# A hybrid decoder layer: operand sums of a branch stored by its attention blocks, and half of a projection's tiles computed as pairs

## The chip, the cores and the metric

The kernel runs on one core of a Trainium2 chip. A core has TensorE (PE, matrix products into the eight banks of PSUM), VectorE (DVE), ScalarE (ACT), GpSimd (POOL) and SyncE (SP), which issues most of the DMA transfers. Each engine executes its own list of instructions in order; semaphores order them among each other. The metric is the device time of one execution in microseconds (us). The time before is 2460.73 us, the median of three runs (2457.89 to 2463.26).

## The reference, cut to what matters

One inference step of a layer on 512 prompt tokens and 8 x 4 sample tokens, 544 columns in all, with a model width of 2048:

```
u = einsum('btd,dc->btc', x, w_in)                       # one wide input projection, cut into parts
q_m, k_m, v_m, o_m, z_m, q_a, k_a, v_a, z_a, g_m, g_a, i_pre, f_pre = parts(u)
h_m = mlstm(q_m, k_m, v_m, i_pre, f_pre)                 # 4 heads of 512, matrix memory; also C, n, m
h_a = sliding_window_attention(q_a, k_a, v_a, sinks)     # 32 heads of 64, window 128
br_m = norm(h_m) * gate(o_m, z_m)                        # branch m
br_a = h_a * silu(z_a)                                   # branch a
y = sig(g_m) * (br_m @ w_proj_m) + sig(g_a) * (br_a @ w_proj_a)
out = layernorm(alpha * x + y @ w_out)
```

The outputs are those of prompt and samples, the new mLSTM state and the last keys and values. The change concerns `br_a @ w_proj_a`, how its operand comes about, and mLSTM, which runs beside it.

## The kernel before

Activations stand transposed: a tile holds 128 model rows on the partitions and T = 544 token columns, 16 such tiles for the width. A product in fp32 precision is made of three matmuls with operands split into a high part (fp32r) and the rest: wh x xh, wh x xl, wl x xh. `split` makes wh on ScalarE (L200) and wl on VectorE (L201) of a loaded weight tile of 128 x 1024; `hilo` does the same with an operand (L245, L246).

There are two ways to compute 256 output rows. Plain (`gemm`, `products`): each tile of 128 output rows takes 16 blocks of the width, three products, two halves of 272 columns, 96 matmuls at L210 into two banks. Paired (`paired`, `half_product`): two tiles together by Strassen's scheme (Winograd's form) over halves of the width, of the columns and of the outputs, seven half products of 16 matmuls at L685 and 8 at L687 instead of eight; it needs four sums of the operand's quarters (s1, n2, n3, s4, made by `operand_sums`) and four of the weights' (`prepare`, L665), and its banks are gathered into the outputs (`gather`, L695 to L714).

The program's stages in order of time: x is loaded and transposed; the input projection runs in pairs up to 1754 us, and beside it, as generators that `tick()` advances by a step after each half product, attention (16 blocks k, each one 128 rows of branch a, written to the DRAM tensor d_bra) and the samples' mLSTM. Then `branch(d_bra, ...)` loads the 16 rows of branch a and splits them into the tiles bh and bl, and a loop over ct = 0 to 15 computes the 16 tiles of w_proj_a, all plain; each is multiplied by the gate's tile (L1560) and stored to d_t. Beside it `mlstm` runs on the prompt's four heads, a generator that is advanced after every second block of a plain tile. Behind mLSTM (from 2010 us) the operand of branch m is loaded and split. From 2122 us w_proj_m is computed with merging, two tiles plain and the rest in pairs, and last w_out.

Of one head of mLSTM these lines matter. `values` (L1417) transposes v and splits it into vh, vl. `decays` (L1449) spreads the decay row over the partitions and makes the exponentials dm on ScalarE (L1458), for which an activation table is loaded. `keys` (L1425) transposes k, VectorE weights it (f, L1427), `hilo` splits it to kwh and kwl, and 24 matmuls at L1438 sum one of four parts of the new state C. `cells` makes the scores (L1470), multiplies them by dm into ph and pl, sums the numerators (L1483) of four row blocks, each into a pair of banks, and `layernorm_rows` normalizes them (its last step reads the banks on ScalarE, L1076); transposes (L1493) and a multiplication by the gate end in d_brm.

What sets the order: the program's text is traced by a scheduler that places instructions on each engine's list by priority (`tc.high_priority`) and by explicit successions (`tc.issue_after`); generators interleave by the number of their yields. The pools set what may overlap: psB (tag sm) and psA (tag bank) have four PSUM banks each.

Of the kernel before, what the change touches and what calls it, by code (L numbers as in the profile page):

```python
# [74 lines left out]
def _build(tc, nc, i, o, es):  # L75
# [3 lines left out]
    def pool(stack, name, bufs, space=None, side=None):  # L79
        kw = {"space": space} if space is not None else {}  # L80
        if space is None:
            kw["side"] = side or "right"
            kw["reuse_waits"] = "tile"
        return stack.enter_context(tc.tile_pool(name=name, bufs=bufs, **kw))
# [9 lines left out]
    psB = pool(es, "psB", 4, PSUM)  # L94
    psA = pool(es, "psA", 4, PSUM)

    dr = pool(es, "dr", 1, bass.MemoryType.DRAM)
# [3 lines left out]
    def nm(s):  # L101
        count[0] += 1
        return f"{s}_{count[0]}"

# [71 lines left out]
    d_y = dr.tile([16, 128, T], F32, name="d_y")  # L176
    d_o = dr.tile([12, 128, T], F32, name="d_o")
# [46 lines left out]
    def gemm(wv, c0, xh, xl, cols=EVEN, raws=(None, None), every=8, prio=0, before=None, parts=(1, 1),  # L224
             ps=None, behind=None):
        ps = ps or mm()
        for half in range(2):
# [9 lines left out]
            products(ps, half, wh, wl, xh, xl, cols, every)  # L237
# [480 lines left out]
    def paired(work, plain=None):  # L718
# [6 lines left out]
        for at, (w, n) in enumerate(steps):  # L725
# [11 lines left out]
            if n == 2 and "early" in w:  # L737
                w["early"]()
            half_product(w, n)
# [22 lines left out]
    def kv_head(kvh):  # L762

# [6 lines left out]
        nc.sync.dma_start(vraw, d_vr[0:SEQ, kvh * 64:kvh * 64 + 64].rearrange("(b p) c -> p b c", p=128))  # L770
        k1, k2 = btile("b1", [128, SEQ], "k1", F32R), btile("b1", [128, SEQ], "k2", F32R)
# [5 lines left out]
    def attention(k, qs, sz, kv):  # L777
# [39 lines left out]
        for a in range(2):  # L817
# [16 lines left out]
            yield  # L834
        for a in range(2):
# [13 lines left out]
        nc.sync.dma_start(d_bra[k][:, 0:SEQ], hT[:])  # L849

# [38 lines left out]
    def attentions():  # L889
# [15 lines left out]
        for k in range(16):  # L905
            if k % 4 == 0:
                kv = kv_head(k // 4)
# [16 lines left out]
    def sample_attention():  # L924
# [118 lines left out]

        PTs = weightsT(0)
# [11 lines left out]
        nc.sync.dma_start(d_bra[:, :, SEQ:T].rearrange("k p t -> p k t"), gas[:])  # L1056

    def layernorm_rows(n, den, em, parts, hn, w):
# [11 lines left out]
        G.tensor_tensor(out=s[:, 5:6], in0=s[:, 4:5], in1=mh[:n, 0:1], op=ALU.pow)  # L1070
# [43 lines left out]
    def sample_prep(h, r):  # L1114
# [72 lines left out]
        A.copy(num, pN[:NS, :])  # L1187
        r.update(kv=load_kv(h, 0), den=den, num=num, qs=qs)
# [23 lines left out]
    def sample_head(h):  # L1212
# [12 lines left out]
        for b in range(NB):  # L1225
# [10 lines left out]
            for j in range(7 if h + b == 0 else 4 + b % 2):  # L1236
# [130 lines left out]
    def branch(src, p, tmp, ahead=()):  # L1367

        hs, los = act_tiles(p, "bh"), act_tiles(p, "bl")

        def steps():
            for k in range(KT):
# [5 lines left out]
                hilo(st[:], hs[k // 4][:, k % 4], los[k // 4][:, k % 4])  # L1378
# [3 lines left out]
    _, bah, bal, g_ = branch(d_bra, act, lambda k: ev(), ahead)  # L1382
# [18 lines left out]
    def f5(dt=F32):  # L1401
        return wA2.tile([128, 512], dt, tag="f5", name=nm("f"))

# [18 lines left out]
    def keys(h, c, kt):  # L1422
# [12 lines left out]
        for b in range(4):  # L1435
            for n, (a, b_) in enumerate(((kwh, vh), (kwh, vl), (kwl, vh))):
                for f, pp in enumerate((p0, p1)):
                    PE.matmul(pp[:, 0:258], a[:, b * 128:b * 128 + 128], b_[:, b, f],  # L1438
# [3 lines left out]
        V.tensor_copy(co[:, 256:512], p1[:, 0:256])  # L1442
# [19 lines left out]
    def cells(h, kh, kl, qh, ql):  # L1462
        hns = []
        for bs_ in ((0,), (1,), (2, 3)):
            for b in bs_:
                n = SEQ - b * 128
                pp = sm()
                for c in range(4):
                    for m, (x_, y_) in enumerate(((kh, qh), (kh, ql), (kl, qh))):
                        PE.matmul(pp[:, 0:n], x_[c][:, b * 128:b * 128 + 128], y_[c][:, b * 128:SEQ],  # L1470
# [4 lines left out]
            yield  # L1475
        for js in ((0, 1), (2,), (3,)):
            for j in js:
                p0, p1 = sm(), sm()
                for b in range(j + 1):
                    off = POFF[b] + (j - b) * 128  # L1480
                    for n, (x_, y_) in enumerate(((ph, vh), (ph, vl), (pl, vh))):
                        for f, pp in enumerate((p0, p1)):
                            PE.matmul(pp[:, 0:258], x_[:, off:off + 128], y_[:, b, f],  # L1483
# [3 lines left out]
                hns.append(hn)  # L1487
            yield
        gt = load4(d_g, h)
# [16 lines left out]
    def mlstm():  # L1506
        for h in range(MH):
            vts = load4(d_v, h)
            spawn(decays(h))
            yield  # L1510
            kts = load4(d_k, h)
# [3 lines left out]
            kh, kl, qh, ql = [], [], [], []  # L1515
            g_ = None
            for c in range(4):
                a, b_ = t5(F32R), t5(F32R)
                V.tensor_copy(a[:], kts[c][:])
                V.tensor_tensor(out=b_[:], in0=kts[c][:], in1=r32(a[:]), op=ALU.subtract)  # L1520
                kh.append(a)
                kl.append(b_)
                n_ = keys(h, c, kts[c])
                next(n_)
                if g_ is not None:
# [4 lines left out]
            for c in range(4):  # L1530
# [449 lines left out]
```

## Time and profile before

| | |
|---|---|
| median of three runs | 2460.73 us (2457.89 to 2463.26) |
| the profiled execution | 2460.73 us, span 2459.0 us |
| mean granted TensorE clock | 0.999 |
| TensorE busy | 2444.3 us (99%), 19466 instructions |
| VectorE busy | 1875.3 us (76%) |
| ScalarE busy | 1217.2 us (50%) |
| GpSimd busy | 510.8 us (21%) |
| bytes moved by DMA | 464.72 MB, 169 GB/s of HBM traffic over the span |

A row of the profile's timeline begins with its start and length in us, then come engine, line, operation, the tiles written and read, their shapes and the count of like instructions; brackets show how long the engine had been idle and what released it. Matmuls are pipelined, and a single one is shown with some 0.28 us; the rate is taken from the starts of a run of them. "L685" is the line of the kernel before; the lines of the changed kernel differ, since text is added ahead of them (L210 becomes L218, L245 L253, L1425 L1472, L1438 L1485, L1483 L1533).

### The profile page before, as it was taken

To read this page: it belongs to the slowest core of one execution; us is meant where nothing else is said; L and a number is where in the kernel's file an instruction comes from. 1 tells how busy PE (TensorE), PEld (TensorE's weight loads), DVE (VectorE), ACT (ScalarE), POOL (GpSimd) and SP (SyncE) were. 2 spreads that over 40 slices of the span, in tenths; PEclk is the share of its full clock that TensorE was granted. 3 is DMA by queue.
4 is the path that set the end of the run, shared out by engine and by line. 5 is a ranking of instruction groups with operands and counts; after the bars stand their busy time and mean duration, and the time that the engine had idled before them with its cause. 6 is when DMAs were issued, how large, how long until landed. Compare 5 with 4: busy or idle time off the path is not lost.

```text
span 2459.0 us, 48851 instructions
## 1 busy us (share of the span) xinstructions
PE 2444.3 (99%) x19466; PEld 2382.7 (97%) x19466; DVE 1875.3 (76%) x2810; ACT 1217.2 (50%) x1999; POOL 510.8 (21%) x479
## 2 busy tenths in 40 slices
PE   8999999999999999999999999999999999999999
PEld 8999999999999999999999999999999999999997
DVE  7778888888888887887877888777865654777656
ACT  6456676676676565443433434434633333344431
POOL 4114334334333330211111221211000000110111
PEclk9999999999999999999999999999999999999999
DMA  6876666666666654577677586676755546888876
GB/s 177 205 173 157 161 162 147 161 163 148 160 156 160 155 153 110 153 226 242 182 252 240 162 246 211 192 228 217 248 175 171 185 155 204 226 222 247 220 221 188
DMA packets 555804, 464.72 MB, mean 189 GB/s; under 512 B 43704, under 2 KB 452584, under 8 KB 555320
## 3 DMA queue, kind: packets, MB, share of 16 engines
q1 hardware_dynamic: 538968, 402.88, 55.5%
q0 software_dynamic: 15696, 57.15, 12.1%
q8 instruction: 153, 2.51, 0.4%
q10 hardware_dynamic: 912, 1.57, 0.2%
q14 instruction: 75, 0.61, 0.1%
HBM read 319.06 MB, written 96.31 MB: 169 GB/s over the span
## 4 chain that ended last, share of the span: by engine, by line
PE 98%; DMA 1%; SPq 1%; DVE 0%; ACT 0%; issue 0%; DVEq 0%; ACTq 0%
PE bank L685 47%; PE bank L687 23%; PE bank L210 13%; PE sm L1438 2%; PE sm L210 1%; PE bank L1250 1%; PE sm L1470 1%; PE sm L795 1%; PE sm L1483 1%; PE sm L841 1%; PE sm L1801 1%; PE sm L821 1%; PE sm L1255 1%; PE bank L409 0%; PE bank L1923 0%; DMA raw<-in_w_in 0%
## 5 line engine op out<-in xcount | busy, mean ns | idle before, releaser
L200 ACT CAST wh<-raw 128x1024 fp32r<-128x1024 f32 x632 | 662.6, 1048 | 843.3 <-PE bank L685 695.7
L201 DVE TENSOR_TENSOR wl<-raw,wh 128x1024 fp32r<-128x1024 f32 x632 | 791.7, 1253 | 201.4 <-ACT wh L200 184.1
L685 PE MATMUL bank<-xk,wh 128*128 128x272 f32 x2336 | 322.0, 289 | 0.0
L665 DVE TENSOR_TENSOR raw<-raw,raw 128x1024 f32<-128x1024 f32 x238 | 301.2, 1267 | 6.6 <-DMA raw<-in_w_in 2.6
L685 PEld LDWEIGHTS bank<-xk,wh 128*128 128x128 f32 x2336 | 302.8, 188 | 2.0 <-issue 1.5
L704 POOL TENSOR_TENSOR ev<-p,ev 128x272 f32<-128x272 f32 x82 | 118.3, 1442 | 437.7 <-ACT ev L703 404.7
L687 PE MATMUL bank<-xk,wl 128*128 128x272 f32 x1168 | 170.1, 288 | 0.0
L685 PE MATMUL bank<-s1h,wh 128*128 128x272 f32 x656 | 169.6, 291 | 0.0
L685 PE MATMUL bank<-n2h,wh 128*128 128x272 f32 x656 | 169.6, 291 | 0.0
L685 PE MATMUL bank<-n3h,wh 128*128 128x272 f32 x656 | 169.3, 290 | 0.2 <-ACT wh L200 0.2
L685 PE MATMUL bank<-n2l,wh 128*128 128x272 f32 x656 | 167.7, 287 | 0.0
L685 PE MATMUL bank<-n3l,wh 128*128 128x272 f32 x656 | 167.6, 288 | 0.0
L685 PE MATMUL bank<-s4h,wh 128*128 128x272 f32 x656 | 167.6, 289 | 0.0
L685 PE MATMUL bank<-s1l,wh 128*128 128x272 f32 x656 | 167.3, 287 | 0.0
L685 PE MATMUL bank<-s4l,wh 128*128 128x272 f32 x656 | 167.0, 287 | 0.0
L687 PEld LDWEIGHTS bank<-xk,wl 128*128 128x128 f32 x1168 | 155.7, 188 | 0.1
L685 PE MATMUL bank<-a11h,wh 128*128 128x272 f32 x584 | 150.3, 289 | 0.0
L685 PE MATMUL bank<-a11l,wh 128*128 128x272 f32 x584 | 149.5, 288 | 0.0
L210 PE MATMUL bank<-bl,wh 128*128 128x272 f32 x704 | 147.6, 288 | 0.0
L210 PE MATMUL bank<-bh,wl 128*128 128x272 f32 x704 | 147.5, 290 | 0.0
L210 PE MATMUL bank<-bh,wh 128*128 128x272 f32 x704 | 147.2, 288 | 0.0
L663 POOL DMA_DIRECT2D raw<-raw x90 | 78.3, 871 | 292.5 <-DVE ev L712 211.6
(506 smaller groups left out, 5679.2 us busy)
## 6 DMA issues: line engine op xcount, KB each, us to landing
raw<-in_w_in SPq DMA_DIRECT2D x296, 512.0 KB
raw<-raw POOLq DMA_DIRECT2D x90, 512.0 KB, 4.9
C<-in_state_mlstm_C SPq DMA_DIRECT2D x32, 1024.0 KB
out<-C SPq DMA_DIRECT2D x64, 512.0 KB
raw<-in_w_proj_a SPq DMA_DIRECT2D x32, 512.0 KB
raw<-in_w_proj_m SPq DMA_DIRECT2D x32, 512.0 KB
raw<-in_w_out SPq DMA_DIRECT2D x32, 512.0 KB
d_v<-ev SPq DMA_DIRECT2D x16, 272.0 KB
```

Of the source, the lines that this page charges most:

```text
L200: state["cast"] = A.copy(wh[:, k:k + n], raw[:, k:k + n])
L201: state["split"] = V.tensor_tensor(out=wl[:, k:k + n], in0=raw[:, k:k + n], in1=r32(wh[:, k:k + n]), op=ALU.subtract)
L210: PE.matmul(ps[f][:, :w], a[:, kk], b(k, c, w), start=(k == 0 and n == 0), stop=(k == 15 and n == 2))
L663: G.dma_start(out=w[out][:], in_=w[b][:], accum_op=ALU.add)
L665: V.tensor_tensor(out=w[out][:], in0=w[a][:], in1=w[b][:], op=ALU.add)
L685: PE.matmul(ps, wh[:, k], x(p, k), start=(first and k == 0 and p == 0), stop=False, skip_group_check=True)
L687: state["end"] = PE.matmul(ps, wl[:, k], x(0, k), start=False, stop=(k == 7), skip_group_check=True)
L704: G.tensor_tensor(out=c22, in0=p1, in1=c11, op=ALU.subtract)
L795: PE.matmul(pp[:, c0 + w0:c0 + 256], qs[a][:, j * 128:j * 128 + 128], kx[:, k0:k0 + 256 - w0], start=(n == 0), stop=(n == 1))
L821: PE.transpose(pt[:, b * 128:b * 128 + 128], s_[:, b, 128:256], ident)
L841: PE.matmul(po[:, b * 128:b * 128 + n], VA[:, b], p_[:, 2 * b:2 * b + n // 128], start=(b == 0 and m == 0), stop=(b == 3 and m == 1), skip ...
L1438: PE.matmul(pp[:, 0:258], a[:, b * 128:b * 128 + 128], b_[:, b, f], start=(b == 0 and n == 0), stop=(b == 3 and n == 2))
```

## The change

1. Attention blocks 8 to 15 load the stored row k - 8 (`sc`), form the four operand sums of the prompt's first and last 240 columns of each half (`branch_sums`: four operations of 128 x 240 on VectorE) and store them to d_sa; the remaining columns, those of the samples and 32 beside, are summed once in the samples' chain and stored to d_ss. The keys and values of the next attention head are loaded one block earlier (`kv_load`).
2. Of w_proj_a the tiles 0 to 5 run plain beside mLSTM, 6 and 7 plain behind it, 8 to 13 as three pairs, 14 and 15 plain. `stored_sums` loads the sums by GpSimd's queue, seven ahead, and splits them (sumh, suml) while 6 and 7 run. The plain tiles beside mLSTM have one pair of banks (psA 2, psB 6); before the pairs the pools return to 4 and 4. Branch m's operand is loaded and split behind the pairs.
3. In mLSTM the next head's v and k are loaded while a head's cells run, the high parts of k are cast on ScalarE instead of VectorE, q is split beside the keys, both read-outs of C run on ScalarE, and the output rows are a generator of their own (`rows_out`). The splits of branch a all stand behind the weights of the last input pair.
4. y's operand sums have three buffers instead of two, and PSUM pools wait by tile.

```diff
+    def psum_pools(n):
+        return pool(esPS, nm("psB"), n, PSUM), pool(esPS, nm("psA"), 8 - n, PSUM)
...
-    def paired(work, plain=None):
+    def paired(work, plain=None, rest=()):
...
+            if at == 4:
+                for _ in rest:
+                    pass
...
+        if k in (3, 7, 11):
+            bp["kv"] = kv_load(k // 4 + 1)
+        if k > 7:
+            sc = scores_tile()
+            nc.sync.dma_start(sc[:, 0:4:2, 0:PC], d_bra[k - 8].rearrange("p (c x) -> p c x", c=2)[:, :, 0:PC])
...
         nc.sync.dma_start(d_bra[k][:, 0:SEQ], hT[:])
+        if k > 7:
+            spawn(branch_sums(sc[:, :, 0:PC], hT[:, 0:PC], hT[:, HT:SEQ], d_sa[k - 8]))
...
+    def branch_sums(t_, r12, r22, to):
+        r11, s1, r21, s4 = (t_[:, j] for j in range(4))
+        V.tensor_tensor(out=s1, in0=r22, in1=r21, op=ALU.subtract)
+        V.scalar_tensor_tensor(r21, r11, -1.0, r21, op0=ALU.mult, op1=ALU.subtract)
+        V.tensor_tensor(out=r11, in0=r11, in1=s1, op=ALU.subtract)
+        V.tensor_tensor(out=s4, in0=r12, in1=r11, op=ALU.subtract)
+        nc.sync.dma_start(to, t_)
+        yield
...
-                    nc.sync.dma_start(st[:], src[k])
-                hilo(st[:], hs[k // 4][:, k % 4], los[k // 4][:, k % 4])
+                    nc.sync.dma_start(st[:], src[k])
+                with tc.issue_after(state["cast"].ins), tc.issue_after(state["split"].ins):
+                    hilo(st[:], hs[k // 4][:, k % 4], los[k // 4][:, k % 4])
...
+    esPS.close()
+    psB, psA = psum_pools(6)
...
         A.copy(co[:, 0:256], p0[:, 0:256])
-        V.tensor_copy(co[:, 256:512], p1[:, 0:256])
+        A.copy(co[:, 256:512], p1[:, 0:256])
...
-                V.tensor_copy(a[:], kts[c][:])
-                V.tensor_tensor(out=b_[:], in0=kts[c][:], in1=r32(a[:]), op=ALU.subtract)
-                kh.append(a)
-                kl.append(b_)
+                two_parts(kts[c], (kh, kl))
                 n_ = keys(h, c, kts[c])
                 next(n_)
+                if c > 1:
+                    two_parts(qts[c - 2], (qh, ql))
...
-    for ct in range(16):
-        sg = c5t()
-        nc.sync.dma_start(sg[:], d_sga[ct])
-        ps = gemm(wa_, ct * 128, bah, bal, every=2)
...
+    def stored_sums(to, p):
...
+        def load(n):
+            t_ = two((tx.tile([128, T], F32, tag="tx", name=nm("tx")) if n % 7 < 4 else ev())[:])[:, :, 0:PC]
+            j = n // 8 * 2
+            G.dma_start(out=t_, in_=d_sa[n % 8][:, j:j + 2])
+            return t_
+
+        with tc.issue_after(state["head"].ins):
+            ahead = [load(n) for n in range(7)]
...
+        for n in range(16):
+            for _ in range(2 if 8 <= n < 12 else 1):
+                yield
+            k, t_ = n % 8, ahead.pop(0)
+            to_ = e if n < 8 else f
+            behind_weights(t_, *(t[k // 4][:, k % 4, :, 0:PC] for t in to_))
+            if k == 4:
+                columns(to_)
...
+            if n + 7 < 16:
+                ahead.append(load(n + 7))
...
+    LEAD_A, PAIR_A, TAIL_A = 6, 8, 14
+    marks = []
+    for ct in range(LEAD_A):
+        marks.append(state.get("cells"))
+        with tc.issue_after(marks[ct - 1].ins) if ct > 1 and marks[ct - 1] else ExitStack():
+            plain_a(ct, every=(1, 2), prio=0 if ct else AHEAD)
+    drain()
...
+    sums_ = stored_sums(SA, act3)
+    next(sums_)
+    spawn(sums_)
+    for ct in range(LEAD_A, PAIR_A):
+        with tc.issue_after(state["cells"].ins):
+            plain_a(ct, every=2, prio=AHEAD)
+    esPS.close()
+    psB, psA = psum_pools(4)
+    XA = operands((bah_, bal_), SA)
+    paired([pair_a(ct) for ct in range(PAIR_A, TAIL_A, 2)], state["split"], rest=sums_)
...
+    for ct in range(TAIL_A, 16):
+        plain_a(ct, every=2, prio=AHEAD)
...
-    tx = pool(esT, "txd", 2)
+    tx = pool(esT, "txd", 3)
     Y = {}
-    spawn(operand_sums(d_y, Y, act3))
+    spawn(operand_sums(d_y, Y, act3, 3))
```

How it moves instructions is shown at three places. First TensorE at the first key matmuls of head 0, before; L210 are products of w_proj_a (bank 21460 and 21461: its tile 1), L1438 the key matmuls, L1425 the transposes of the next k.

```order
L210 MATMUL bank_21461<-bh_21103,wh_21643 128x272
L210 MATMUL bank_21460<-bl_21107,wh_21643 128x272
L210 MATMUL bank_21461<-bl_21107,wh_21643 128x272
L1438 MATMUL sm_21366<-vh,kwh_21335 128x258
L1438 MATMUL sm_21367<-vh,kwh_21335 128x258
L1438 MATMUL sm_21366<-vl,kwh_21335 128x258
L1425 MATMUL sm_21413<-cc,t_21214 128x128 x4
```

The same place after; bank 21244 and 21245 are tile 0, bank 21538 is tile 1.

```order
L218 MATMUL bank_21244<-bh_21173,wl_21353 128x272
L218 MATMUL bank_21245<-bh_21173,wl_21353 128x272
L1485 MATMUL sm_21440<-vh,kwh_21408 128x258
L1485 MATMUL sm_21441<-vh,kwh_21408 128x258
L1485 MATMUL sm_21440<-vl,kwh_21408 128x258
L1485 MATMUL sm_21441<-vl,kwh_21408 128x258
L1472 MATMUL sm_21487<-cc,t_21294 128x128 x4
L218 MATMUL bank_21538<-bh_21167,wh_21542 128x272
```

The key matmuls moved from the middle of tile 1 to the end of tile 0: 96 product matmuls now stand ahead of them in this stage, 154 before. Second, ScalarE ahead of the first kwh (t: high parts of k and q; vh: of v; dm: the exponentials), before:

```order
L200 CAST wh_21643<-raw_21641 128x1024
L1458 ACTIVATE dm<-f_21228,colT_90 128x128 x6
L245 CAST t_21538<-t_21316 128x512
L245 CAST vh<-sm_21296 128x4x128
L245 CAST t_21542<-t_21318 128x512
L245 CAST kwh_21335<-f_21333 128x512
```

and after:

```order
L253 CAST t_21552<-t_21296 128x512
L253 CAST vh<-sm_21368 128x4x128
L1500 COPY f_21327<-sm_21324 128x384
L1505 ACT_TABLE_LOAD
L1505 ACTIVATE dm<-f_21326,colT_90 128x128 x4
L253 CAST t_21567<-t_21391 128x512
L1505 ACTIVATE dm<-f_21327,colT_90 128x128 x6
L253 CAST t_21608<-t_21393 128x512
L253 CAST kwh_21408<-f_21406 128x512
```

Between the last bh of branch a and the first kwh ScalarE's list now holds seven casts t instead of two. Third, TensorE where a plain tile follows a plain tile with nothing between, before (banks 24320, 24321, then 24467, 24468: two pairs of the four banks):

```order
L210 MATMUL bank_24320<-bh_21104,wl_24384 128x272
L210 MATMUL bank_24321<-bh_21104,wl_24384 128x272
L210 MATMUL bank_24467<-bh_21101,wh_24471 128x272
L210 MATMUL bank_24468<-bh_21101,wh_24471 128x272
L210 MATMUL bank_24467<-bl_21105,wh_24471 128x272
```

and after (tile 6 in banks 23982 and 23983, tile 7 begins in 24134; the pool has two banks):

```order
L218 MATMUL bank_23982<-bh_21173,wl_24057 128x272
L218 MATMUL bank_23983<-bh_21173,wl_24057 128x272
L218 MATMUL bank_24134<-bh_21167,wh_24138 128x272
L218 MATMUL bank_24134<-bl_21168,wh_24138 128x272
L218 MATMUL bank_24134<-bh_21167,wl_24139 128x272
```

Tile 7 begins with one half alone, in one of the two banks that tile 6 has just filled.

163 lines of the change are left out of this document (116 added, 47 removed).

## The prediction

> **What bounds the kernel now.** I read the page first: the span, the engines' busy time, and the chain that ended last by engine and line.
>
> ```profile
> span 2459.0 us, 48851 instructions
> PE 2444.3 (99%) x19466; PEld 2382.7 (97%) x19466; DVE 1875.3 (76%) x2810; ACT 1217.2 (50%) x1999; POOL 510.8 (21%) x479
> PE 98%; DMA 1%; SPq 1%; DVE 0%; ACT 0%; issue 0%; DVEq 0%; ACTq 0%
> PE bank L685 47%; PE bank L687 23%; PE bank L210 13%; PE sm L1438 2%; PE sm L210 1%; PE bank L1250 1%; PE sm L1470 1%; PE sm L795 1%; PE sm L1483 1%; PE sm L841 1%; PE sm L1801 1%; PE sm L821 1%; PE sm L1255 1%; PE bank L409 0%; PE bank L1923 0%; DMA raw<-in_w_in 0%
> ```
>
> TensorE is the path: 98% of the chain, 70% of it pair matmuls (L685, L687) and 13% plain tiles (L210). Two things can therefore move the time: how many matmuls there are, and new waits of TensorE. Next the list of TensorE's waits (in total, times, longest), then the busy time of each engine in four stretches.
>
> ```profile
> PE sm L295 <- DMA cc<-in_consts: 3.4, 1, 3.4
> ...
> PE sm L1255 <- DMA VB<-d_kv: 1.9, 1, 1.9
> PE bank L210 <- DVE wl L201: 1.3, 1, 1.3
> ```
> ```profile
> 400.00:800.00 400.00, 400.00 (x3222) 400.00 (x3221) 333.86 (x497) 267.62 (x507) 147.17 (x113) 1.00 0.66 156
> 1740.00:1770.00 30.00, 30.00 (x242) 29.95 (x242) 25.95 (x39) 20.51 (x34) 1.49 (x3) 1.00 1.00 331
> 1770.00:2010.00 240.00, 240.00 (x1913) 237.98 (x1912) 144.78 (x373) 85.94 (x168) 12.35 (x18) 1.00 0.49 161
> 2010.00:2125.00 115.00, 115.00 (x923) 114.97 (x922) 69.69 (x121) 42.80 (x68) 5.31 (x7) 1.00 0.75 228
> ```
>
> The columns behind the length are PE, PEld, DVE, ACT, POOL, granted clock, DMA share, GB/s. In the stage that the change rewrites (1755 to 2122) TensorE never waits; VectorE works 60% of it and ScalarE 36%. So there is nothing to win there but matmuls, and every new wait is a loss. The chain gives the rate of TensorE in long pieces:
>
> ```profile
> 1756.58 13.71 PE bank L210 x110
> ...
> 1803.50 1.45 PE sm L1483 x12
> ...
> 1820.93 1.09 PE sm L1493 x10
> ...
> 2012.45 109.59 PE bank L210 x878
> ```
>
> A product matmul takes 109.59/878 = 0.1248 us, a numerator matmul 0.121, a transpose 0.109.
>
> **The matmuls removed: -9.0 us.** A plain tile is 16 blocks x 3 products x 2 halves = 96 matmuls. Two of them become a pair of 7 half products of 24, 168 in all, of the same 272 columns. Three pairs save 3 x 24 = 72 matmuls, 72 x 0.1248 = 9.0 us. All else that TensorE does keeps its count. Nothing excludes that these matmuls count in full: the chain is TensorE there.
>
> **h0's first key matmuls: +4.0 us.** Head 0 of mLSTM now runs beside 96 product matmuls before its first key matmul, where it had 154, counted in the order of the instructions (110 of them are the chain's piece at 1756.58).
>
> When TensorE gets there: the last pair's matmuls are over when the first transposes of before start,
>
> ```profile
> 1754.37 0.60 PE L1417 MATMUL sm<-cc,t 128*128 128x128 f32 x4
> ```
>
> then 96 x 0.125 + 24 transposes x 0.109 + the decay row of about 0.3 = 15.0 us: 1769.4. When kwh is ready: ScalarE works in order, and these are its rows of before.
>
> ```profile
> 1750.55 2.29 ACT L245 CAST bh<-pf 128x544 fp32r<-128x544 f32 x4 [1.95 <-PE bank L685]
> 1752.74 1.04 ACT L200 CAST wh<-raw 128x1024 fp32r<-128x1024 f32 x1
> ...
> 1759.57 0.65 ACT L1310 ACTIVATE ev<-ev 128x544 f32<-128x544 f32 x1
> 1761.91 1.05 ACT L200 CAST wh<-raw 128x1024 fp32r<-128x1024 f32 x1 [1.69 <-issue]
> 1762.90 1.57 ACT L245 CAST vh<-sm 128x512 fp32r<-128x512 f32 x3
> 1766.22 0.48 ACT L1453 COPY f<-sm 128x384 f32<-128x384 f32 x1 [1.75 <-DVE f L1451]
> 1766.72 1.28 ACT L1458 ACT_TABLE_LOAD   x1
> 1768.01 1.28 ACT L1458 ACTIVATE dm<-f,colT 128x128 f32<-128x128 f32 x4
> ...
> 1770.14 1.86 ACT L1458 ACTIVATE dm<-f,colT 128x128 f32<-128x128 f32 x6
> 1771.90 0.60 ACT L245 CAST t<-t 128x512 fp32r<-128x512 f32 x1
> ...
> 1773.41 1.14 ACT L245 CAST kwh<-f 128x512 fp32r<-128x512 f32 x2
> ```
>
> By the order after, ahead of kwh stand seven operand casts t (two before) and four more casts of bh, which before ran earlier, between the last pair's products:
>
> ```profile
> 1737.37 1.81 ACT L245 CAST bh<-pf 128x544 fp32r<-128x544 f32 x3
> ```
>
>  The first four bh fit into the 1.95 us idle and the slot at 1750.55, the next wh ends near 1752.4, then: 4 bh, 4 bh, sigmoid, wh, 4 bh, sigmoid (3 x 2.2 + 2 x 0.6 + 1.0 = 8.8, to 1761.2), 4 t, 2 vh, wh, vh, t, vh (5 casts of t at 0.55, 4 of vh at 0.52, 1.0: 5.8, to 1767.0), copy and table load (1.8, to 1768.8), the exponentials with a t between and one behind (1.2 + 1.8 + 1.1, to 1772.9), kwh 0.55: 1773.4. The wait is 1773.4 - 1769.4 = 4.0 us. Bounds: if the first four bh end 0.9 us earlier, at 1750.6, and TensorE comes 0.6 later by small waits of its own, 2.5; if they get no early slot, the list ends at 1774.8 (5.4). I take the sum itself: it leaves ScalarE no idle time, as the rows of before with their two idles of 1.7 us don't. Tile 1 can't fill in: its bank is one of only two in this stage, and VectorE reads it out behind the f that feeds kwh.
>
> One rule speaks against this term. In the rows above the table load occupies 1.28 us and the next exponential starts 1.29 us after its start, so I sum 1.28. The Trainium skill ("ScalarE: Activation LUTs", What ACT_TABLE_LOAD costs) adds a drain of about 1.38 us to every switch; with it the wait would be an estimated 5.4 us and the time 2459.3. The rows show the copy ahead starting 0.50 us before the load, so no such drain; the rows decide.
>
> **Numerators of head 3: +1.0 us.** Heads 0 to 2 have 21 to 27 product matmuls ahead of their last numerator; head 3 has none: 60 matmuls (6, 12, 18 and 24 for the four row blocks) in a row, each block with two of six banks. Block 3 needs block 0's pair back. It starts 36 x 0.121 = 4.4 us after block 0, whose matmuls take 0.7, and whose banks ScalarE reads last:
>
> ```profile
> 1801.71 0.41 PE L1483 MATMUL sm<-vh,pl 128*128 128x258 f32 x2
> ```
> ```profile
> 1805.57 1.02 ACT L1076 ACTIVATE t<-sm,lns 128x256 f32<-128x256 f32 x2 [3.56 <-DVE lns L1072]
> ```
>
> From the last matmul to free banks: 1806.6 - 1802.0 = 4.6. So 0.7 + 4.6 - 4.4 = 0.9, and a semaphore: 1.0 (0 if block 0's chain is quicker without other work; 2 if a wl of 1.2 falls into it).
>
> **Tile to tile on two banks: +1.2 us.** The plain tiles of this stage own one pair of banks, where they had two. After, tile 7 stands right behind tile 6 and wants its first bank, which VectorE must read out first:
>
> ```profile
> 1768.83 0.78 DVE L1560 TENSOR_TENSOR c<-bank,c 128x272 f32<-128x272 f32 x2
> ```
>
> One read is 0.4, with the matmul's drain and semaphores some 0.8 (0.4 to 1.6, if a wl is in the way). At the other joints mLSTM's matmuls stand between; 0.4 for all of them.
>
> **Costed at nothing.** The eight blocks' sums: 32 operations of 240 columns on VectorE, eight loads and eight stores on SyncE's queue.
>
> ```profile
> L342 DVE TENSOR_TENSOR r<-sm,r 128x240 f32<-128x240 f32 x8 | 3.2, 394 | 0.0
> ```
>
> 4 x 0.39 = 1.6 us for a block; VectorE is 84% busy there (333.86 of 400), so it stays under 88% and the weights stay ahead. If that cover is gone, each block costs up to 1.6, 12.6 in all. Waits they add: the first sum waits on VectorE for GpSimd's last product of the block, and weight parts queue behind it. The 20 splits of stored sums (ScalarE 0.55, VectorE 0.62 each) run beside tiles 6 and 7, 24 us of TensorE, with VectorE's own 15 us of weights and reads there. Sixteen key casts and sixteen read-outs go from VectorE to ScalarE, which has 64% free. A third buffer for y's tiles, the sample chain's moved steps (two earlier, two fewer later) and the key loads moved ahead change no order on TensorE.
>
> Sum: -9.0 + 4.0 + 1.0 + 1.2 = -2.8. The profiled execution took 2460.73 us (span 2459.0), which is the median too (2457.89 to 2463.26): 2457.9. About 0.2%, 4.9 us, is what a measurement of this kernel can tell from no change.
>
> **Rivals.**
> *The waits don't come:* kwh early enough and banks free, so all 72 matmuls are won: 2451.7; with half of the waits 2454.8. For it: no wait at all in this stage before. Against: ScalarE's list is in order and longer by nine casts. 0.27.
>
> *The wait halves the clock.* After the first 3.4 us without work TensorE was slow, after 3.0 us later it was not:
>
> ```profile
> 3.44 4.53 PE L295 MATMUL sm<-cc 128*128 128x128 f32 x20 [3.44 <-DMA cc<-in_consts]
> 7.76 2.14 PE L328 MATMUL sm<-cc,xr 128*128 128x128 f32 x16
> 9.74 0.60 PE L331 MATMUL bank<-cc,xs 128*128 128x128 f32 x4
> 13.33 0.63 PE L328 MATMUL sm<-cc,xr 128*128 128x128 f32 x4 [2.99 <-DMA xr<-in_x_prompt]
> 13.71 0.37 PE L210 MATMUL bank<-a11h,wh 128*128 128x272 f32 x1
> ```
> ```profile
> 0.00:10.00 10.00, 6.56 (x39) 1.00 0.85 235
> ```
>
> 20 transposes in 4.32 us (0.216 each), then 16 in 1.98 (0.124); behind the wait of 2.99, 4 in 0.38. The granted clock (1.00 in the second fence, PE alone) doesn't show it; the spacing does. A wait of 4.0 lies beyond both; slow matmuls for 4.3 us would cost 2.2 more: 2460.1. 0.12. The Trainium skill ("TensorE: Matmul & The Clock Gate", Part 1) has the same rule with a window of about 3.4 us; the trace agrees at both rows.
>
> *Stored sums late, slower:* the first pair's second half product needs half of the sums, read back by GpSimd's queue seven ahead. A load like them:
>
> ```profile
> tx<-d_brm POOLq DMA_DIRECT2D x8, 544.0 KB, 7.2
> ...
> tx<-d_y POOLq DMA_DIRECT2D x8, 544.0 KB, 5.3
> ```
>
> Two rounds of loads are 14.4 us of the 24 that tiles 6 and 7 cover. If the loads start 15 us late, 5 us of them and the splits behind (5 us) stand open: 2468. It ends slower from 7.7 us in the open. For it: a buffer frees only when both engines have split it, and VectorE has the pair's weights too. 0.21.
>
> **How the numbers follow.** Forecast 0.40, its own range 2455 to 2461; waits away 0.27; clock 0.12; sums late, or the same in the attention blocks, 0.21. Faster by over 0.2% (under 2455.8): 0.26 from the waits away and 0.08 from the forecast, 0.34. Slower (over 2465.6): 0.19. Between: 0.47. The range reaches to the first rival's end, 2451.5, and into the last, 2466.0.
>
> **What would show it.** In the changed profile: 72 fewer product matmuls; a wait of TensorE at L1485 on kwh of 2.5 to 5.4 us and of no other head; waits of about 1 us at L1533 and L218; TensorE's spacing behind the first wait (0.125 or 0.25); no wait at the first pair's L693 on suml. Wrong would be: waits of TensorE in the attention blocks, at the first pair, or a chain with less than 97% of TensorE.

## The result, and the profile after

The changed kernel takes 2472.87 us (median, 2471.99 to 2474.5) where the kernel before, run beside it, takes 2459.4 (2457.89 to 2463.26): a ratio of 1.0048, with an interval of 1.0036 to 1.006. It is half a per cent slower. The forecast was 2457.9 with a range up to 2466.0, so it was wrong, and on the wrong side. The two profiled executions differ in the same way: spans of 2471.1 and 2459.0 us, 12.1 apart. The page after, its lines on the span, the engines and the chain:

```profile
span 2471.1 us, 48979 instructions
PE 2443.2 (99%) x19394; PEld 2379.0 (96%) x19394; DVE 1903.9 (77%) x2857; ACT 1247.9 (50%) x2069; POOL 523.2 (21%) x504
PE 91%; issue 3%; DMA 3%; DVE 2%; ACT 0%; SPq 0%; POOL 0%; ACTq 0%; DVEq 0%; POOLq 0%
```

The 72 matmuls are gone (19466 before, 19394 now), and yet TensorE's busy time is only 1.1 us shorter, where 72 x 0.1248 is 9.0: the matmuls that are left are in part slower ones. Its share of the chain has fallen from 98% to 91%. The list of TensorE's waits (in all, times, longest) says who took its place:

```profile
PE sm L1297 <- DMA VB<-d_kv: 5.7, 2, 3.3
PE sm L1485 <- issue: 3.5, 1, 3.5
...
PE sm L994 <- DMA kb<-in_state_attn_k: 1.7, 1, 1.7
PE bank L218 <- DVE wl L209: 1.4, 2, 1.2
PE sm L1212 <- DVE nT L1208: 0.9, 1, 0.9
PE sm L1533 <- ACT t L1116: 0.9, 1, 0.9
PE sm L1485 <- ACT kwh L253: 0.7, 2, 0.5
...
PE bank L218 <- DVE c L1694: 0.5, 1, 0.5
```

They fall into two places. L1485 (keys), L1533 (numerators) and L218 belong to w_proj_a with mLSTM beside it, where the forecast looked. L994 (the samples' attention), L1212, a further 0.6 at L1225 and the first of the two waits at L1297 (all the samples' mLSTM) lie between 898 and 1061 us, in the input projection, where it costed everything at nothing.

Aligning the pair matmuls of both traces by their number gives the account: +0.1 us up to 898 us, **+10.0 between 898 and 1061**, +0.9 from there to the last input pair, +0.1 from 1754 to 2100 (9.0 of matmuls gained, 9.1 of waits and slow clock lost), +1.9 for two waits on wl at 2104.8 and 2117.3, -1.5 since the wait on wl that the kernel before has at 2294 is gone, +0.6 behind the last matmuls. The sum is 12.1. Five sixths of the loss thus come from one stretch of 163 us.

This is how TensorE passes the worst place there, the samples' matmuls with VB. Its timeline before (start, length, line, tiles, count):

```profile
1047.16 0.50 PE L1255 MATMUL sm<-VB,Ab 32*128 32x512 f32 x4
1047.59 0.39 PE L685 MATMUL bank<-n3h,wh 128*128 128x272 f32 x1
...
1050.71 0.29 PE L685 MATMUL bank<-s4h,wh 128*128 128x272 f32 x1
```

and after:

```profile
1054.59 0.88 PE L1297 MATMUL sm<-VB,Ab 32*128 32x512 f32 x4 [3.27 <-DMA VB<-d_kv]
1055.40 0.59 PE L693 MATMUL bank<-n3h,wh 128*128 128x272 f32 x1
...
1060.79 0.29 PE L693 MATMUL bank<-s4h,wh 128*128 128x272 f32 x1
```

The load of VB comes 3.27 us late. Behind it the 24 matmuls with n3 take 5.39 us (1055.40 to 1060.79) where they took 3.12 before (1047.59 to 1050.71), and the four with VB 0.81 instead of 0.43: 2.7 us more, for a clock that fell during the wait. Busy time and granted clock in windows of the same trace (length, PE busy, clock, DMA share, GB/s):

```profile
1055.00:1062.00 7.00, 7.00 (x38) 0.61 0.91 273
1785.00:1788.00 3.00, 3.00 (x17) 0.58 0.44 128
```

**Why VB is late.** VB holds what an earlier step of the samples' chain stored, so its load is the last link of a chain of transfers. SyncE's timeline at the start of that chain, before:

```profile
1006.26 0.37 SPq L1056 DMA_DIRECT2D d_bra<-gas  x1
1006.72 1.91 SPq L1111 DMA_DIRECT2D C<-in_state_mlstm_C  x1
...
1031.11 0.53 SPq L1106 DMA_DIRECT2D VB<-d_kv  x1
```

and after:

```profile
1008.67 0.37 SPq L1091 DMA_DIRECT2D d_bra<-gas  x1
1018.79 0.34 SPq L879 DMA_DIRECT2D d_ss<-kb  x1
1021.46 0.38 SPq L1151 DMA_DIRECT2D C<-in_state_mlstm_C  x1
...
1047.64 0.55 SPq L1146 DMA_DIRECT2D VB<-d_kv  x1
```

Before, the first load of the samples' mLSTM (C) starts 0.46 us after the samples' branch is stored. After, 12.8 us lie between the two, and the store of the samples' sums, d_ss, stands in the gap; everything down to VB (16.5 us late) shifts with it. The order of instructions on SyncE, with the semaphores that each waits for, tells what joins them:

```
L879 DMA d_ss<-kb 128x1024 [waits DMAHW2_49,DVE_49]
L1346 DMA d_g<-ev_12388 128x544 [waits DMAHW3_49,Pool_49]
L1151 DMA C_12534<-in_state_mlstm_C 128x4x512 [waits DMAHW4_49,DMAHW2_49,PE_49]
L1159 DMA qs_12536<-d_q 128x4x32 [waits DMAHW5_49,DMAHW0_49]
```

Each transfer waits for its own queue (2, 3, 4, 5 in turn); the load of C waits for queue 2 as well, that of d_ss. The sums are formed in kb, a tile of the samples' attention. The samples' mLSTM takes the space of that pool for its own tiles, and may not do so before the store has read kb. SyncE's own waits in that stretch name the store too:

```profile
SPq L879 <- DVE kb L878: 2.5, 1, 2.5
...
SPq L1151 <- DMA d_ss<-kb: 0.8, 1, 0.8
```

Only the last 0.8 us of the 12.8 is SyncE standing at the load of C and waiting for d_ss to land. The rest is what stands ahead of that load in SyncE's list, which is in order: a weight load that waits 7.0 us, the store itself, which waits 2.5 us for VectorE, and d_g with 1.1.

The store waits for six small operations. One copy is made early; the other five stand on VectorE's list between weight parts:

```profile
1009.82 0.29 DVE L1094 COPY kb<-gas 128x256 f32<-128x256 f32 x1
1010.50 1.22 DVE L209 TENSOR_TENSOR wl<-raw,wh 128x1024 fp32r<-128x1024 f32 x1
...
1018.34 0.42 DVE L878 TENSOR_TENSOR kb<-kb 128x256 f32<-128x256 f32 x1
```

The five take some 2.0 us by themselves; from the start of the first to the end of the last it is 9 us. Block 15's store of its sums (d_sa) stands in the same place ahead of the samples' attention: the load of qraw, which opens it, starts at 919.88 behind `d_sa<-s` at 916.98, where before it started at 911.89. That could be the wait on kb at L994, 1.7 us.

**The stage that was predicted.** The keys of head 0, and ScalarE ahead of them:

```profile
1783.85 0.55 PE L1485 MATMUL sm<-vh,kwh 128*128 128x258 f32 x2 [3.52 <-issue]
```
```profile
1777.38 0.48 ACT L1500 COPY f<-sm 128x384 f32<-128x384 f32 x1 [0.60 <-DVE f L1498]
1777.88 1.28 ACT L1505 ACT_TABLE_LOAD   x1
1779.18 1.28 ACT L1505 ACTIVATE dm<-f,colT 128x128 f32<-128x128 f32 x4
...
1783.14 0.61 ACT L253 CAST kwh<-f 128x512 fp32r<-128x512 f32 x1
```

The wait is 3.52 us; it ends with the cast of kwh, in front of which ScalarE has idled for only 0.6 us since 1766. The next exponential starts 1.30 us behind the start of the table load. The Trainium skill ("ScalarE: Activation LUTs", What ACT_TABLE_LOAD costs) adds a drain of about 1.38 us to every switch of tables; this trace, like the one before, shows none.

### The profile page after: what moved, and what is told of

It reads as the page before. It is cut to its first block, busy times and chain, and to the rows that moved or that the text cites. A ratio compares the mean times of both kernels' runs of the same rounds, so it can differ in the third digit from the quotient of the medians.

```text
span 2471.1 us, 48979 instructions
## 1 busy us (share of the span) xinstructions
PE 2443.2 (99%) x19394; PEld 2379.0 (96%) x19394; DVE 1903.9 (77%) x2857; ACT 1247.9 (50%) x2069; POOL 523.2 (21%) x504
## 4 chain that ended last, share of the span: by engine, by line
PE 91%; issue 3%; DMA 3%; DVE 2%; ACT 0%; SPq 0%; POOL 0%; ACTq 0%; DVEq 0%; POOLq 0%
PE bank L693 46%; PE bank L695 23%; PE bank L218 8%; PE sm L1485 2%; PE sm L218 1%; PE sm L1517 1%; PE sm L808 1%; PE bank L1292 1%; PE sm L1533 1%; PE sm L859 1%; DVE wl L209 1%; PE sm L1944 1%; PE sm L1297 1%; DMA VB<-d_kv 1%; PE sm L834 1%
## 5 line engine op out<-in xcount | busy, mean ns | idle before, releaser
L208 ACT CAST wh<-raw 128x1024 fp32r<-128x1024 f32 x641 | 671.5, 1048 | 834.7 <-PE bank L693 707.6
L209 DVE TENSOR_TENSOR wl<-raw,wh 128x1024 fp32r<-128x1024 f32 x641 | 801.1, 1251 | 204.8 <-ACT wh L208 183.3
L673 DVE TENSOR_TENSOR raw<-raw,raw 128x1024 f32<-128x1024 f32 x244 | 309.9, 1271 | 7.8 <-issue 2.5
L671 POOL DMA_DIRECT2D raw<-raw x96 | 83.5, 870 | 323.9 <-DVE ev L720 209.5
L693 PEld LDWEIGHTS bank<-n3h,wh 128*128 128x128 f32 x656 | 124.5, 190 | 2.8 <-issue 1.5
L693 PEld LDWEIGHTS bank<-s1h,wh 128*128 128x128 f32 x656 | 123.2, 188 | 1.6 <-issue 1.0
L693 PEld LDWEIGHTS bank<-n2h,wh 128*128 128x128 f32 x656 | 123.3, 188 | 1.5 <-issue 1.4
```

The source lines that it names most:

```text
L208: state["cast"] = A.copy(wh[:, k:k + n], raw[:, k:k + n])
L209: state["split"] = V.tensor_tensor(out=wl[:, k:k + n], in0=raw[:, k:k + n], in1=r32(wh[:, k:k + n]), op=ALU.subtract)
L671: G.dma_start(out=w[out][:], in_=w[b][:], accum_op=ALU.add)
L673: V.tensor_tensor(out=w[out][:], in0=w[a][:], in1=w[b][:], op=ALU.add)
L693: PE.matmul(ps, wh[:, k], x(p, k), start=(first and k == 0 and p == 0), stop=False, skip_group_check=True)
```

## The experiments

Each time stands beside runs of the kernel before on the same chip; the ratio is to those. Line numbers shift a little between the kernels.

### What moved the samples' chain?

Three theories: the store that holds the pool (A), the moved steps of the chain (B), or VectorE, which does the sums too late (C).

**yields_back** undoes the moved steps alone.

```diff
-        for _ in range(0 if h else 2):
-            yield
...
-            for j in range(5 if h + b == 0 else 4 + b % 2):
+            for j in range(7 if h + b == 0 else 4 + b % 2):
```

> The changed kernel with the sample chain's seven steps back where they were (none ahead of the first load of VB, seven instead of five behind). Theory A, the samples' pools wait for the store of the new sums d_ss, and everything of the sample chain comes late by that: nothing changes, 2471 to 2475 us, TensorE still waits about 3.3 us for head 0's VB. Rival B, the two steps ahead of VB's load make it late: that wait goes, and with it the slow matmuls behind it, 2464 to 2468 us.

Measured: 2471.99 us, ratio 1.0046 (1.0031 to 1.0061), not to be told from the changed kernel. TensorE's waits:

```profile
PE sm L1295 <- DMA VB<-d_kv: 6.1, 2, 3.3
```

The wait of 3.3 stays, and the load of C still starts 2.67 us behind the store of d_ss (1020.65 and 1017.98). Theory B falls.

**sums_first** gives the sums' VectorE operations priority over the weights, so that the store would come earlier.

```diff
+        with tc.high_priority(offset=AHEAD):
+            V.tensor_tensor(out=s1, in0=r22, in1=r21, op=ALU.subtract)
...
+        with tc.high_priority(offset=AHEAD):
+            V.tensor_copy(t_[:, 0], rim[:, 0:8])
```

> The changed kernel with all branch sums (blocks 8 to 15 and the samples') at high priority on VectorE. Theory A: the store d_ss leaves about 6 us earlier (1012 instead of 1018.8), the pools open as much earlier, TensorE's wait for VB of 3.3 us goes: 2464 to 2469 us. Rival B: VB stays late, 2471 to 2475. Rival C, the sums' 14 us on VectorE make the weights late: slower than the changed kernel.

Measured: 2473.51 us, 1.005 (1.0034 to 1.0067), the wait for VB 3.5. This run missed its aim, as SyncE's timeline shows:

```profile
1017.86 0.34 SPq L880 DMA_DIRECT2D d_ss<-kb  x1
1020.53 0.38 SPq L1153 DMA_DIRECT2D C<-in_state_mlstm_C  x1
```

The store moved by 0.9 us, as the whole of VectorE's list did, and that list is in the same order: priority alone did not bring the operations past the weights. So it says nothing for or against an earlier store; what it does repeat is the fixed distance of 2.67 us from store to load.

**sample_sums_late** takes the store away: the samples' columns stay in d_bra, and their sums are formed beside tiles 6 and 7, from 32 columns loaded again. The sums no longer use kb, and d_ss does not exist; the same sums are made.

```diff
-        t_ = left[:, 0:1024].rearrange("p (j k t) -> p j k t", j=4, k=8)
-        V.tensor_copy(t_[:, 0], rim[:, 0:8])
-        V.tensor_copy(t_[:, 2], gas[:, 0:8])
-        for _ in branch_sums(t_, rim[:, 8:16], gas[:, 8:16], d_ss):
-            pass
...
+            for r_, k, c in ((r11, 0, PC), (r22, 8, SEQ), (r21, 0, SEQ), (r12, 8, PC)):
+                nc.sync.dma_start(r_, d_bra[k:k + 8, :, c:c + 32].rearrange("k p t -> p k t"))
...
+            if n == 4:
+                with tc.issue_after(state["cast"].ins), tc.issue_after(state["split"].ins):
+                    column_sums()
```

> The changed kernel with the samples' and rim columns summed beside tiles 6 and 7 instead of ahead of the samples' pools, no d_ss. Theory A: state and operands of the samples' head 0 are loaded at about 1009 instead of 1021, the waits at L1212, L1225 and VB (4.8 us) and the 2.2 us of slow matmuls go, and the rest of the 10.1 us that the stretch from 1027 to 1061 lost: 2462 to 2465 us. Rival B: 2471 to 2475. Rival C, the attention blocks' own sums slow the stage: at most 2 us less.

Measured: 2464.8 us, 1.0016 (1.0006 to 1.0025); the span 2462.5, 8.6 shorter than the changed kernel's. SyncE's timeline, and a window of TensorE at VB:

```profile
1008.34 2.22 SPq L1141 DMA_DIRECT2D C<-in_state_mlstm_C  x1
...
1032.89 0.53 SPq L1136 DMA_DIRECT2D VB<-d_kv  x1
```
```profile
1045.00:1062.00 17.00, 17.00 (x137) 1.00 0.64 192
```

The transfers are back within 2 us of their places before, TensorE waits nowhere between 1000 and 1075 us, and its clock is full. Theory A holds for the larger part of the loss: the samples' sums where the change put them cost 8.6 us of the 12.1 in the profiled executions, and about 7.9 by the ratios of all runs. The run takes the store, its operations on VectorE and its place in SyncE's list away together. That C waits for the landing of the store rests on the semaphore, on SyncE's wait for it and on the fixed 2.67 us. How much a store of the same sums out of a buffer outside that pool would cost, no run tests.

**no_block15**, on top of it, leaves out block 15's sums (rows 7 and 15 take block 14's).

```diff
-        if k > 7:
+        if 7 < k < 15:
...
-            G.dma_start(out=t_, in_=d_sa[n % 8][:, j:j + 2])
+            G.dma_start(out=t_, in_=d_sa[min(n % 8, 6)][:, j:j + 2])
```

> The kernel with the samples' sums late, and without the sums of attention block 15: rows 7 and 15 of branch a take block 14's sums, which leaves out a part of the computation. If the store of block 15's sums holds the attention's pools, as d_ss held the samples': the samples' attention loads its operands at about 912 instead of 920, TensorE's wait of 1.5 us for kb goes, 1.5 to 2 us less: 2462 to 2464. Rival, other traffic makes kb late: the wait stays, 2464 to 2466.

Measured: 2463.85 us, 1.0013 (1.0004 to 1.0022), span 2460.9. The load that opens the samples' attention starts 1.5 us behind its place before the change, where it was 8.0 late, and TensorE's wait on kb falls from 1.5 to 0.4:

```profile
913.42 0.53 SPq L972 DMA_DIRECT2D qraw<-d_qa  x1
```
```profile
PE sm L993 <- DMA kb<-in_state_attn_k: 0.4, 1, 0.4
```

So block 15's sums, where they stand, cost 1.1 us in the wait and 1.6 in the span of the profiled executions; by the ratios the two kernels can't be told apart. That the mechanism is the same is not shown: the changed kernel's SyncE has no wait for the landing of d_sa between 905 and 925 us, so the places in its list may be all of it.

### What are the pairs worth?

**plain_again**, on sample_sums_late, computes tiles 8 to 13 plain, while the sums are still loaded and split.

```diff
-    paired([pair_a(ct) for ct in range(PAIR_A, TAIL_A, 2)], state["split"], rest=sums_)
+    drain()
+    for ct in range(PAIR_A, TAIL_A):
+        plain_a(ct, every=2, prio=AHEAD)
```

> The kernel with the samples' sums late, and the six tiles 8 to 13 plain again instead of three pairs (the sums are still made, stored, loaded and split). What the pairs are worth by themselves: 72 matmuls of 0.1248, 9.0 us, less the 1.3 us that the first pair waits for sumh: 7 to 9 us more than the kernel with the sums late, 2471 to 2474. Rival, the pairs cost VectorE and the DMA queues so much that they are worth under 4 us: 2466 to 2468.

Measured: 2477.75 us, 1.0062 (1.0047 to 1.0077); span 2475.5, 13.0 over sample_sums_late (about 11 by the ratios), where 7 to 9 had been expected. TensorE's waits of the two kernels differ most in one line each; here plain_again, then sample_sums_late:

```profile
PE bank L217 <- DVE c L1693: 4.6, 2, 4.1
```
```profile
PE bank L692 <- ACT sumh L252: 1.3, 1, 1.3
```

A plain tile waits 4.1 us for banks that VectorE, busy with the splits, reads out late; the clock behind it is 0.60 for 4 us, another 1.6. So 13.0 is near 9.0 + 4.1 + 1.6 - 1.3 = 13.4, or 12.2 less two small waits (0.8 and 0.4) that only sample_sums_late has: the pairs' 9.0 is there to within about 1 us. The wait on sumh is the stored sums' lateness, 1.3 us and not the 7 or more of the rival.

### What makes kwh late, and can the wait be taken away?

**k_cast_vector**, on the changed kernel, returns head 0's high parts of k to VectorE: four casts fewer on ScalarE.

```diff
-                two_parts(kts[c], (kh, kl))
+                two_parts(kts[c], (kh, kl), A.copy if h else V.tensor_copy)
```

> The changed kernel with the high parts of head 0's k cast on VectorE, as before the change. If ScalarE's list makes the first kwh late: four casts of 0.55 less ahead of it, the wait of 3.5 us at L1485 falls to 1.3 to 2.0, and the matmuls behind it run at full speed (1.9 us more): 2468 to 2470. If VectorE's f makes it late: the wait stays above 3 us, 2472 to 2474.

Measured: 2469.98 us, 1.0037 (1.0025 to 1.0049), an interval that overlaps that of the changed kernel.

```profile
PE sm L1485 <- issue: 2.3, 1, 2.3
```

The wait shrinks by 1.2 us, where the four casts took 2.17 in a row on ScalarE in the changed kernel. VectorE's list is nearly as full: in the changed kernel its f for kwh ends at 1782.0, 1.1 before the cast. In this run ScalarE idles 2.3 us ahead of the table load, for VectorE's f (L1498), where it idled 0.6. So ScalarE's list sets the wait in the changed kernel, and VectorE takes its place as soon as that list is shorter. The clock still fell (0.51 from 1785 to 1788), against what was expected.

**h0_later**, on sample_sums_late, starts head 0 four steps later (the expectation says three), so that 154 products stand ahead of its first key matmul as in the kernel before.

```diff
-        for _ in range(4):
+        for _ in range(8):
             yield
```

> The kernel with the samples' sums late, and mLSTM's head 0 begun three steps later (eight instead of four ahead of the load of k), so that 154 product matmuls stand ahead of its first key matmul, as before the change, instead of 96. If head 0's wait of 3.5 us and the 1.9 us of slow matmuls behind it come from too few products ahead of ScalarE's list: both go, tile 0 to tile 1 on two banks costs 0.8 back: 4 to 5 us less than the kernel with the sums late, 2458 to 2461. Rival, the waits only move, to the banks or to head 1's keys: 2463 or more.

Measured: 2466.36 us, 1.0024 (1.0014 to 1.0034), span 2463.3, 0.8 over sample_sums_late. The window over the place shows the wait and the slow clock gone, the list of waits what came instead:

```profile
1755.00:1810.00 55.00, 55.00 (x436) 1.00 0.57 186
```
```profile
PE sm L1462 <- DMA t<-d_k: 2.1, 2, 1.1
PE bank L217 <- DVE wl L208: 2.0, 2, 1.8
```

The distance in products is what makes the wait, as predicted. But the kernel is not faster for it, and the expected 4 to 5 us did not come; the rival did: TensorE waits for k and weights (and 1.7 us for banks) in the place of kwh, and behind a wait of 1.77 us at 2098 the clock falls after all.

**bh_early**, on sample_sums_late, frees branch a's splits from the rule that they stand behind the last pair's weights.

```diff
+                with ExitStack() as place:
+                    if k >= free:
+                        place.enter_context(tc.issue_after(state["cast"].ins))
+                        place.enter_context(tc.issue_after(state["split"].ins))
...
+    (bah_, bal_), bah, bal, g_ = branch(d_bra, act, lambda k: ev(), ahead, free=16)
```

> The kernel with the samples' sums late, and branch a's splits free again to run between the last input pair's weights. Four casts of bh (2.3 us) leave ScalarE's list ahead of head 0's kwh. If that list makes kwh late: the wait at the first key matmul falls from 3.5 to 1.2 to 2.0 us, 2 to 4 us less than the kernel with the sums late: 2460 to 2463. Rival, VectorE's chain to f makes it late: the wait stays over 3 us, 2463 to 2466.

Measured: 2462.75 us, 1.0008 (0.9998 to 1.0018), with the wait at 2.7 us and slow matmuls behind it (clock 0.50 from 1775 to 1778). The wait falls less far than expected (1.2 to 2.0 us), and the time can't be told from that of sample_sums_late.

**bh_early_k_cast** joins the two edits:

```diff
+    (bah_, bal_), bah, bal, g_ = branch(d_bra, act, lambda k: ev(), ahead, free=16)
...
-                two_parts(kts[c], (kh, kl))
+                two_parts(kts[c], (kh, kl), A.copy if h else V.tensor_copy)
```

> The same with head 0's four casts of k on VectorE as well. If ScalarE's list is the cause: the wait at the first key matmul is under 0.8 us and no matmul behind it is slow, 4.5 to 5.6 us less than the kernel with the sums late: 2459 to 2461. If the four casts of 0.42 on VectorE make f late instead: a wait of 1 to 2 us stays, 2461 to 2463.

Measured: 2465.18 us, 1.002 (1.001 to 1.003), with a longer wait, and now plainly on the cast:

```profile
PE sm L1478 <- ACT kwh L252: 3.6, 1, 3.6
```

A miss: the gains do not add. The scheduler put one more weight cast (1.04 us at 1774.45) ahead of kwh.

**best** adds to it block 15's sums formed late from the stored rows.

```diff
-        if k > 7:
+        if 7 < k < 15:
...
+            for r_, k, c in ((q11, 7, 0), (q22, 15, HT), (q21, 7, HT), (q12, 15, 0)):
+                G.dma_start(out=r_, in_=d_bra[k, :, c:c + HT])
...
+            V.tensor_tensor(out=q22, in0=q22, in1=q21, op=ALU.subtract)
...
-    tx = pool(esB2, "txb", 4)
+    tx = pool(esB2, "txb", 3)
```

> The same, and block 15's sums made beside tiles 6 and 7 too, from the stored rows, so that nothing of the change holds the attention's pools. 1.5 to 2 us less than without that, less up to 1 us that TensorE waits longer for sumh at the first pair: 2457 to 2460 us, within 0.2% of the kernel before or just under it.

Measured: 2467.14 us, 1.0023 (1.0014 to 1.0033), again with 3.7 us on kwh and a new 2.0 at the first pair on wh; the wait on kb fell to 0.8 as meant. A miss too.

**later_bh_early** joins sample_sums_late, bh_early and a start three steps later.

```diff
-        for _ in range(4):
+        for _ in range(7):
             yield
```

> The kernel with the samples' sums late and branch a's splits free, and head 0 begun three steps later (seven instead of four): about 155 product matmuls ahead of its first key matmul. Both causes of head 0's wait are off, its 2.7 us and the 1.2 us of slow matmuls go, with up to 0.8 us back where tile 1 follows tile 0 on two banks, and up to 2 us if the heads behind it find their k or their weights late, as in the kernel with head 0 later alone: 2457 to 2461 us. Rival, each such step only hands the wait on: 2462 or more.

Measured: 2458.67 us, 0.9992 (0.9983 to 1.0001), span 2456.2:

```profile
PE sm L1478 <- ACT kwh L252: 1.3, 1, 1.3
```

The wait of 3.5 is gone; one of 1.3 on kwh comes behind 1800 us instead, and the clock stays full at the first keys (1.00 from 1770 to 1790).

**later_block15** adds the late sums of block 15 (as in best), and one step in an early generator with them.

```diff
-        for _ in range(6):
+        for _ in range(7):
             yield
...
-        if k > 7:
+        if 7 < k < 15:
```

> The same, and block 15's sums made beside tiles 6 and 7 from the stored rows. The wait for kb of 1.6 us goes as it did without block 15's sums; the first pair may wait up to 2 us for weights or sums: 2456 to 2460 us. If the first pair's wait takes all of it: equal to the kernel without this edit.

Measured: 2459.66 us, 0.9992 (0.9984 to 1.0001); span 2455.6, kb 0.9, VB 2.1. Both are level with the kernel before within what can be told; if they are faster, it is by under 0.2%. The repaired change is 0.56% faster than the one made, but no version measured beats the kernel before beyond doubt.

## Why the prediction was wrong

**The step that failed** is in "Costed at nothing": that the sums cost only VectorE's time, "32 operations of 240 columns on VectorE, eight loads and eight stores on SyncE's queue", and that "the sample chain's moved steps (two earlier, two fewer later) and the key loads moved ahead change no order on TensorE". The forecast counted the eight blocks' sums and left out the ninth, that of the samples' columns, with its load, six operations and store. Above all it asked what the stores wait for, and not who waits for the stores. The tile that the sums use belongs to a pool whose space the next stage takes. The store of d_ss held it, C started 12.8 us later behind the branch's store, and TensorE lost 10.0 us between 898 and 1061. The runs show 8.6 us for the samples' sums (sample_sums_late) and 1.6 for block 15's (no_block15, too little to be sure of), both from the profiled executions. The moved steps themselves cost nothing that can be told, as the step said (yields_back); the order on TensorE did change, since the scheduler placed the late chain later, and in the samples' mLSTM it is that of before again with sample_sums_late. Of the signs that the prediction named for being wrong, the chain with less than 97% of TensorE came (91%); waits came in the samples' attention and mLSTM, if not in the attention blocks.

**-9.0 for the matmuls:** right; 72 fewer, and plain_again is 13.0 slower, some 3 to 4 of it by its own waits and slow clock.

**h0's keys, +4.0:** 3.5 of wait, within the bounds of 2.5 to 5.4, with the named cause: the cast list of ScalarE is the last to end (its rows above, and k_cast_vector), and the number of products ahead decides (h0_later). Not foreseen: head 3's keys wait too, 0.7 in all, against "of no other head".

**Numerators, +1.0,** and **tile to tile, +1.2:** 0.9 of idle time for the first; 0.5 of idle time, 0.7 with the matmul's own delay, for the second. The first is right and the second at the low end of its bounds.

**The rival of the clock** (0.12) came true twice: at the keys some 1.9 us, where it was priced at 2.2, and behind VB 2.7, where no wait had been foreseen. That its price was near is partly luck, since the rule behind it, slow beyond 3.4 us of waiting and not at 3.0, does not hold (see the end).

**The rival of the late sums** (0.21) had the sign, and "or the same in the attention blocks" came near the place, but its mechanism did not act. No wait of TensorE on sumh appears in the changed kernel. VectorE's load in the attention blocks rose as said, from 333.86 to 338.24 us in the 400 from 400 to 800, and TensorE stayed busy there:

```profile
400.00:800.00 400.00, 400.00 (x3222) 400.00 (x3221) 338.24 (x518) 266.42 (x508) 143.82 (x113) 1.00 0.69 165
1770.00:2010.00 240.00, 234.47 (x1844) 231.23 (x1843) 152.34 (x372) 114.38 (x234) 24.65 (x38) 0.99 0.58 184
```

The second row is the stage of mLSTM: TensorE idles 5.5 us of 240 where it idled none, about as the sum had it. With the clock's 1.9, another 1.7 of late matmul starts that no wait in the list accounts for, and the waits on wl behind it (1.9 new, 1.5 gone) the stage came to +0.5 instead of -2.8. That error alone would have stayed inside the range; the samples' chain did not.

## What to carry to other kernels

A store out of a borrowed buffer is part of the release of that buffer's pool: ask who takes the space next, and follow that stage's first load down to the last transfer that an engine waits for. Small operations on an engine that is 77% busy over the run, and 97% in the 10 us in question, cost little of its time but may take 9 us from the first to the last, which matters as soon as a store or a pool hangs on the last of them. When two engines' lists are nearly equally full ahead of a join, taking work off one moves the wait only until the other one ends.

## What the runs showed of the hardware

The clock falls behind much shorter waits than I had reckoned with. Spacing or granted clock was about half for some 3 us and more behind waits of TensorE of 3.52, 3.27, 2.72 (VB's second wait in sample_sums_late), 2.67 (bh_early), 2.34 (k_cast_vector), 2.01 (VB's second wait in sums_first) and 1.77 us (h0_later, at 2098.23). It was full behind 1.78 in yields_back, at 2107.17 and for the same kind of tile. Windows behind these two, h0_later and then yields_back:

```profile
2098.00:2102.00 4.00, 3.77 (x19) 0.59 0.75 236
```
```profile
2107.00:2111.00 4.00, 3.83 (x30) 1.00 0.79 250
```

It was full behind 2.43 as well (VB's second wait in the changed kernel):

```profile
1590.22 0.50 PE L1297 MATMUL sm<-VB,Ab 32*128 32x512 f32 x4 [2.43 <-DMA VB<-d_kv]
...
1590.88 0.29 PE L693 MATMUL bank<-n2l,wh 128*128 128x272 f32 x1
1591.00 0.29 PE L693 MATMUL bank<-n2h,wh 128*128 128x272 f32 x1
```

Here the spacing is 0.12 to 0.13 at once. So between 1.77 and 2.99 us the length of a single wait does not decide it: 1.77 slowed the matmuls in one run and 1.78 did not in another, nor had 2.99 in the kernel before. The Trainium skill ("TensorE: Matmul & The Clock Gate", Part 1) speaks of a window of about 3.4 us that runs freely; a wait's place against such a window could explain the mixture, but slow matmuls behind 1.77 us fit only if a window with some work in it can also count as idle. No run here tests that. For a sum, a wait of 1.8 us or more is better priced with a possible loss behind it, up to the 2.7 us seen behind VB.
